# First sums in a tile of their own and weights cast ahead of h at the start; final sums ahead of x1's tiles and row factors read from PSUM at the end

## The chip, the core and the metric

The kernel runs on one core of a Trainium2 chip. The core has a matrix engine (TensorE, "PE" in the profile, with its weight loads as "PEld"), VectorE ("DVE"), ScalarE ("ACT"), GpSimd ("POOL") and SyncE ("SP", used here only to issue DMA transfers). Each engine works through its own queue in order; semaphores tie the queues together. SBUF is the on-chip memory of 128 partitions; PSUM is the accumulator memory that TensorE writes. The metric is the device time of one execution in microseconds; before the change it is 2057.03, the median of three runs (2055.79 to 2059.26).

## What is computed

One step of a layer for 128 context tokens and 256 latent tokens, 384 rows of 2048 channels in all, in float32:

```
mod = silu(cond) @ w_ada + b_ada
sh1, sc1, ga1, sh2, sc2, ga2 = split(mod, 6)
h = rmsnorm(x, norm_pre_mix) * (1 + sc1) + sh1
m, s_f, s_b = mixer(h, ...)
x = x + ga1 * rmsnorm(m, norm_post_mix)
h = rmsnorm(x, norm_pre_ffn) * (1 + sc2) + sh2
ff = (silu(h @ w_ffn_gate) * (h @ w_ffn_up)) @ w_ffn_down
x = x + ga2 * rmsnorm(ff, norm_post_ffn)
```

The mixer (gated linear attention beside a Fourier branch) and the feed-forward products fill the middle of the kernel. The change touches the first two lines of h at the start and the last line at the end.

## The kernel before

Everything is kept transposed: a tile is 128 channels (partitions) by 384 tokens, and there are 16 such tiles of x, numbered k or kb (T = 384, KT = 16, D = 2048). To keep float32 accuracy with the faster rounded type, each operand is split into a rounded part hi and a remainder lo, and a product is made of three matmuls: hi by hi, hi by lo, lo by hi. For a weight tile the split is a copy on ScalarE (`ACT.copy(hi, raw)`, line 224) and a subtraction on VectorE (line 225); for activations it is `split_act` (lines 283 and 284). The order of the instructions on TensorE, ScalarE, VectorE and GpSimd is the order of the program text; SP's is that too in the last part. The bookkeeping of semaphores is automatic: a tile is reused only when its readers are done, and a tile in PSUM is used by one engine at a time.

**Start (lines 316 to 511, "stage A").** SP loads x (`xT`), small columns, and then for each block kb the two halves of a slab of w_ada (128 x 2048 floats each, five buffers), the v weights (`raw`, 128 x 1024, two buffers) and 256 columns of the q weights (`xraw`, two buffers). Behind the loads of blocks 0 and 1 stand five small loads (`wlr`, `coef`, `bgate`, `gnorm`, `selr`, lines 357 to 361), of which `wlr` is used in this stage, by `lrprod`, and the others later. ScalarE squares the 16 tiles of x, VectorE adds them up in two accumulators qsA. TensorE does 10 warming matmuls into `px` (line 432), then sums over the channels (`tok_sum`, line 291: one-column matmuls with ones) into columns of `pmod`, which is a part of the PSUM tile `pgm`. Another part of pgm is `pgv`, in which `gemv` (line 374, 16 matmuls for a block) collects the block's modulation sums. `msx` (line 435) scales the sums, `rsqrt` makes the row factor r0, `rows` (lines 309 and 310) multiplies the identity by it on VectorE three times and spreads it over the partitions with a matmul by ones into px, and ScalarE copies px to `rstd`.

In block kb the loop over kb then does, on TensorE, gemv(kb); up to four products that go through px and are flushed by VectorE (`xprod` for two groups of q columns, line 409, and every fourth block `lrprod`, line 416); `vprod` (line 391) in three parts of six matmuls, for block kb-1: part 0 is hi by hi, part 1 h's hi by the weight's lo, part 2 h's lo by the weight's hi; and a pair of two-column matmuls that folds `ev`, ScalarE's copy of pgv (line 466), into the shift and scale `mods` of the block (lines 476 and 480). VectorE multiplies x by rstd (line 462, into `scr`, called hf), applies mods (line 482), and ScalarE and VectorE split the result into A_hi and A_lo (hT). The block's weights are split after that (`split_w`), and used in the next block.

**End (from line 1205).** In the last chunk of the down projection, `down` adds each product to the accumulator and squares it; the squares are added up in qs[0] on VectorE one tile late (`late`, line 1176), the last one is added by a second matmul source. Then TensorE puts x1's tiles 4, 5 and 8 into PSUM by the identity (`put`, line 1208), sums the squares (line 291), puts 9 and 14, spreads the row factor with `rows` into `prow`, and puts 15. `rr` is ScalarE's copy of prow in SBUF. Each output tile is x1 + acc * factor. Six tiles (4, 5, 8, 9, 14, 15) get the sum on TensorE: VectorE multiplies, TensorE adds the product to py, ScalarE copies py back and stores. Six (0, 1, 6, 7, 12, 13) are multiplied and added on VectorE and stored by SP. Four (2, 3, 10, 11) are multiplied and added on GpSimd and stored by SP. All but the first product read rr from SBUF.

## Time and profile before

| | |
|---|---|
| median of three runs | 2057.03 us |
| profiled execution | 2056.04 us, of which its span 2054.3 us |
| TensorE busy | 2024.7 us, 99% of the span |
| VectorE busy | 1274.9 us, 62% |
| ScalarE busy | 770.1 us, 37% |
| GpSimd busy | 45.4 us, 2% |
| DMA | 373.94 MB moved |

The span runs from the first to the last instruction of the profiled execution; the rest of its time, 1.74 us, lies around it. In a timeline a row has the start and the duration in microseconds, then engine, line, operation, output and inputs, shape and count; a bracket behind it gives the idle time of the engine before it and what ended that. Neighbouring instructions of one kind are merged in a row. In the table of windows each row is a stretch; behind its length come busy time and instructions of TensorE, its weight loads, VectorE, ScalarE and GpSimd, then the granted clock of TensorE as a share of full speed, the DMA engines' mean busy share, and GB/s.

### The profile page before, as it was taken

What the parts mean: (1) busy time and instruction counts of PE and PEld (TensorE: products, weight loads), DVE (VectorE), ACT (ScalarE), POOL (GpSimd) and SP (SyncE); (2) the same over time, 40 slices, a digit from 0 to 9 for tenths busy, and PEclk for the clock granted to TensorE, in tenths of its full rate; (3) what the DMA queues carried; (4) which work ended last, traced back from release to release, by engine and by line L of the source; (5) the groups of instructions that cost most, each with busy time, mean ns of one, the idle gap of its engine ahead of it and who ended that gap; (6) DMA issues with size and microseconds to landing.
All of it is one profiled execution on the core that took longest, in us unless ns stands there. A gap on an engine that the chain in (4) does not pass through costs nothing.

```text
span 2054.3 us, 30097 instructions
## 1 busy us (share of the span) xinstructions
PE 2024.7 (99%) x12214; PEld 1956.1 (95%) x12214; DVE 1274.9 (62%) x1663; ACT 770.1 (37%) x1143; POOL 45.4 (2%) x52
## 2 busy tenths in 40 slices
PE   8999999999999999999999999999999999999998
PEld 5779999999999999978999999999999999999996
DVE  5669787898667778867444555553545454544346
ACT  3233545453346544445333322222222322222234
POOL 0000000000000000022000000000000000000001
PEclk9999999999999999999999999999999999999998
DMA  9978677767646785532444444443444444433332
GB/s 387 354 261 274 206 238 230 240 222 259 202 158 209 257 282 183 187 113 93 154 144 152 146 144 154 144 146 125 150 144 147 151 144 148 148 125 124 123 133 83
DMA packets 112563, 373.94 MB, mean 182 GB/s; under 512 B 13860, under 2 KB 32484, under 8 KB 108328
## 3 DMA queue, kind: packets, MB, share of 16 engines
q1 hardware_dynamic: 111560, 370.84, 52.8%
q8 instruction: 96, 1.57, 0.3%
q10 hardware_dynamic: 864, 1.18, 0.2%
q14 instruction: 43, 0.35, 0.1%
HBM read 358.34 MB, written 13.63 MB: 181 GB/s over the span
## 4 chain that ended last, share of the span: by engine, by line
PE 96%; DVE 2%; DMA 1%; ACT 1%; issue 0%; SPq 0%; DVEq 0%; ACTq 0%
PE pmm L257 66%; PE pdn L257 18%; PE pv L391 3%; PE pf L257 2%; PE pgm L374 1%; PE px L409 1%; DVE yE L1227 0%; PE po L603 0%; PE pmm L1131 0%; DMA Clo<-in_xT 0%; PE pr L538 0%; DMA slab<-in_w_ada 0%; DVE z L1090 0%; PE dl L603 0%; PE px L844 0%
## 5 line engine op out<-in xcount | busy, mean ns | idle before, releaser
L257 PE MATMUL pmm<-A_hi,whi 128*128 128x384 f32 x2480 | 832.6, 336 | 0.0
L257 PE MATMUL pmm<-A_hi,wlo 128*128 128x384 f32 x2480 | 828.9, 334 | 0.0
L257 PE MATMUL pmm<-A_lo,whi 128*128 128x384 f32 x2480 | 828.8, 334 | 0.0
L225 DVE TENSOR_TENSOR wlo<-raw,whi 128x1024 fp32r<-128x1024 f32 x433 | 529.0, 1223 | 433.8 <-ACT whi L224 432.9
L224 ACT CAST whi<-raw 128x1024 fp32r<-128x1024 f32 x436 | 457.7, 1050 | 587.4 <-PE pmm L257 223.2
L257 PEld LDWEIGHTS pmm<-A_hi,whi 128*128 128x128 f32 x2480 | 465.6, 188 | 3.4 <-issue 1.8
L257 PEld LDWEIGHTS pmm<-A_lo,whi 128*128 128x128 f32 x2480 | 465.7, 188 | 0.2
L257 PEld LDWEIGHTS pmm<-A_hi,wlo 128*128 128x128 f32 x2480 | 465.6, 188 | 0.0
L530 DVE SCALAR_TENSOR_TENSOR adacc<-adaw,spad,adacc 128x1024 f32<-128x1024 f32 x240 | 296.9, 1278 | 0.6 <-DMA adaw<-in_w_ada 0.3
L257 PE MATMUL pdn<-hid_hi,whi 128*128 128x384 f32 x704 | 235.2, 334 | 0.0
L257 PE MATMUL pdn<-hid_hi,wlo 128*128 128x384 f32 x704 | 235.1, 334 | 0.0
L257 PE MATMUL pdn<-hid_lo,whi 128*128 128x384 f32 x704 | 235.1, 334 | 0.0
L257 PEld LDWEIGHTS pdn<-hid_hi,whi 128*128 128x128 f32 x704 | 132.2, 188 | 0.4 <-issue 0.4
L257 PEld LDWEIGHTS pdn<-hid_lo,whi 128*128 128x128 f32 x704 | 132.2, 188 | 0.0
L257 PEld LDWEIGHTS pdn<-hid_hi,wlo 128*128 128x128 f32 x704 | 132.2, 188 | 0.0
L283 ACT CAST hid_hi<-hfE 128x384 fp32r<-128x384 f32 x44 | 22.6, 513 | 161.6 <-DVE hfE L1154 161.6
L1154 DVE TENSOR_TENSOR hfE<-sg,pmm 128x384 f32<-128x384 f32 x44 | 24.4, 555 | 82.2 <-PE pmm L257 81.6
L1146 ACT ACTIVATE sg<-pmm 128x384 f32<-128x384 f32 x44 | 21.6, 492 | 133.5 <-PE pmm L257 133.5
L1171 DVE TENSOR_TENSOR Blo<-Blo,pdn 128x384 f32<-128x384 f32 x72 | 39.5, 553 | 46.6 <-PE pdn L257 46.6
L1171 DVE TENSOR_TENSOR Bhi<-Bhi,pdn 128x384 f32<-128x384 f32 x72 | 39.0, 549 | 34.0 <-PE pdn L257 34.0
L257 PE MATMUL pmm<-o_hi,whi 128*128 128x384 f32 x128 | 42.8, 335 | 0.0
L257 PE MATMUL pmm<-o_lo,whi 128*128 128x384 f32 x128 | 42.8, 334 | 0.0
(301 smaller groups left out, 1556.9 us busy)
## 6 DMA issues: line engine op xcount, KB each, us to landing
adaw<-in_w_ada SPq DMA_DIRECT2D x128, 512.0 KB
raw<-in_w_g SPq DMA_DIRECT2D x88, 512.0 KB
raw<-in_w_u SPq DMA_DIRECT2D x88, 512.0 KB
raw<-in_w_d SPq DMA_DIRECT2D x88, 512.0 KB
slab<-in_w_ada SPq DMA_DIRECT2D x32, 1024.0 KB
raw<-in_w_gate SPq DMA_DIRECT2D x64, 512.0 KB
raw<-in_w_in SPq DMA_DIRECT2D x44, 512.0 KB
raw<-in_w_out SPq DMA_DIRECT2D x32, 512.0 KB
```

The source lines that it names most:

```text
L224: ACT.copy(hi, raw)
L225: eng.tensor_sub(lo, raw, hi.bitcast(F32))
L257: PE.matmul(dst, w[wi][:, k * n + n0 : k * n + n0 + P], x[xi][:, k0 + k, :], start=first and k == 0 and j == 0, stop=last and k == kts - 1 ...
L283: ACT.copy(hi, src)
L374: PE.matmul(pgv[q : q + 32, :], spad[:, k, :], slab[k // (KT // 2)][:, k % (KT // 2), :], start=k < 4, stop=k >= KT - 4,)
L391: PE.matmul(pv[2 * t + g], hT[x_][:, kb, t * P : (t + 1) * P], w_[:, g * 512 : (g + 1) * 512], start=kb == 0 and j == 0, stop=kb == KT - 1 ...
L409: PE.matmul(px, w_[:, u * P : (u + 1) * P], hT[x_][:, kb, :], start=j == 0, stop=j == 2)
L530: DVE.scalar_tensor_tensor(acc[:, c, :], w, spad[:, k, c : c + 1], acc[:, c, :], op0=ALU.mult, op1=ALU.add,)
L1146: ACT.activation(sgs[j], p, AF.Silu)
L1154: DVE.tensor_mul(hf, sgs.pop(j), p)
L1171: DVE.tensor_add(acc(k), acc(k), p)
```

## The change

At the start:

- The five small loads are issued in block 4, behind the loads for block 5, instead of ahead of block 2's.
- There are 11 warming matmuls. The channel sums go to px instead of pmod, with 64 columns of ones instead of one; msx reads px. The row factor is spread by three 128x128 matmuls that take r0, broadcast along its columns, as weights and the identity as moving operand; the three scalings on VectorE go.
- gemv's second half of block 0 stands right behind these. In blocks 1 and 2 gemv comes behind vprod's part 0 and the first xprod; part 1 is then made ahead of the pair of two-column matmuls.
- ev is copied ahead of the weights' casts, and the casts ahead of A_hi; the subtractions that make the weights' lo parts come behind A_lo (in block 0, the one for the q columns stays early).
- lrprod runs in blocks 6, 10 and 14 instead of 4, 8 and 12.

At the end:

- The last square but one is not added to qs[0] by VectorE but summed by TensorE as a second source; the last square is summed apart, and VectorE joins the two sums.
- One x1 tile is put ahead of the sums, one ahead of the row factor and one behind it; the other three follow one by one behind the products.
- The row factor is spread as at the start. VectorE's products all read prow in PSUM. Where VectorE also makes the sum, the product goes to a PSUM tile, `pys`. rr is used by GpSimd alone, whose eight operations are issued without a break.
- TensorE has tiles 0, 4, 8, 1, 5, 9; GpSimd 2, 6, 10, 14; VectorE 3, 7, 11, 12, 13, 15.

```diff
-    def split(at=None, eng=DVE, hold=False):
+    def split(at=None, eng=DVE, hold=False, defer=None):
...
                 ACT.copy(hi, raw)
-                eng.tensor_sub(lo, raw, hi.bitcast(F32))
+                sub = lambda: eng.tensor_sub(lo, raw, hi.bitcast(F32))
+                sub() if defer is None else defer.append(sub)
...
-        def split_w(kb):
-
-            split()
+        def split_w(kb, defer):
+
...
-            ACT.copy(hi, raw)
-            DVE.tensor_sub(lo, raw, hi.bitcast(F32))
+
+            if kb == 0:
+                ACT.copy(hi, raw)
+                DVE.tensor_sub(lo, raw, hi.bitcast(F32))
+            split(defer=defer)
+            if kb:
+                ACT.copy(hi, raw)
+                defer.append(lambda: DVE.tensor_sub(lo, raw, hi.bitcast(F32)))
             return take(), (hi, lo)
...
-        SP.dma_start(wlr, a["w_lr"])
...
+        def load_later():
+            SP.dma_start(wlr, a["w_lr"])
...
-        warm(px, 10)
-        tok_sum(pmod[:, 8:11], *qs)
+        warm(px, 11)
+
+        for t in range(3):
+            for n, q in enumerate(qs):
+                PE.matmul(
+                    px[:, t * P : t * P + 64], q[:, t * P : (t + 1) * P], ones[:, 0:64], start=n == 0, stop=n == 1,
+                )
         gemv(0, range(KT // 2))
-        DVE.tensor_scalar_mul(msx, pmod[:, 8:11], 1.0 / D)
+        DVE.tensor_scalar_mul(msx, px[:, 0:T:P], 1.0 / D)
         r0 = pa.tile([P, 3], F32, name="r0")
         rsqrt(r0, msx, 1.0)
-        rows(pb, px, r0, 1)
+        for t in range(3):
+            PE.matmul(px[:, t * P : (t + 1) * P], r0[:, t : t + 1].to_broadcast([P, P]), ident, start=True, stop=True)
+        gemv(0, range(KT // 2, KT))
...
+                if kb == 4:
+                    load_later()
+
+            wait = kb in (1, 2)
+            if kb and not wait:
+                gemv(kb)
             todo = []
-            if kb and kb % 4 == 0:
-                todo.append(lrprod(kb - 4))
+            if kb > 4 and kb % 4 == 2:
+                todo.append(lrprod(kb - 6))
...
+            if wait:
+                vprod(kb - 1, prev[0], (0,))
             pe_x(0)
             hf = scr[:, kb % 8, :]
             DVE.tensor_mul(hf, xn(kb), rstd)
-            if kb == 0:
-                prev = split_w(0)
+            flushes[0]()
+            if wait:
+                gemv(kb)
             ev = pb.tile([P, 256], F32, tag="ev", name="ev")
             ACT.copy(ev, pgv)
-            flushes[0]()
+            lag = []
+            new = split_w(kb, lag)
             if kb:
-                vprod(kb - 1, prev[0], (0,))
+                vprod(kb - 1, prev[0], (1 if wait else 0,))
...
             split_act(hT[0][:, kb, :], hT[1][:, kb, :], hf)
...
+            for sub in lag:
+                sub()
...
-                    if late:
+                    if late and k < KT - 1:
                         DVE.tensor_add(qs[0], qs[0], late.pop())
...
+        put(pe_ks[0], psm, "mm")
+        pst = pss.tile([P, 8], F32, tag="side", name="pstE")
+        prow = pss.tile([P, T], F32, tag="side", name="prowE")
+
+        last_sq = late.pop()
+        tok_sum(pst[:, 0:3], qs[0], *late)
+        tok_sum(pst[:, 4:7], last_sq)
+        r3 = pe.tile([P, 3], F32, name="r3", bufs=1)
+        DVE.tensor_copy(r3, pst[:, 0:3])
+        DVE.tensor_add(r3, r3, pst[:, 4:7])
+        rsqrt(r3, r3, 1.0 / D)
+        put(pe_ks[1], psm, "mm")
...
+        pys = pss.tile([P, T], F32, tag="side", name="pys")
...
+        def on_pool(k):
+            y = pe.tile([P, T], F32, tag="t1", name="yP", bufs=3)
+            POOL.tensor_mul(y, acc(k), rr)
+            POOL.tensor_add(x1(k), x1(k), y)
+
+        def on_pe(n):
+            k = pe_ks[n]
+            y = pe.tile([P, T], F32, tag="hf", name="yE", bufs=4)
+            DVE.tensor_mul(y, acc(k), prow)
+            PE.matmul(py[k], ident, y, start=False, stop=True)
+            if n + 3 < len(pe_ks):
+                put(pe_ks[n + 3], pss, "side")
+            ACT.copy(x1(k), py[k])
+            store(k, ACT)
+
+        for k in pool_ks:
+            on_pool(k)
+        on_pe(0)
+        for n, k in enumerate(dve_ks):
+            DVE.tensor_mul(pys, acc(k), prow)
+            if n + 1 < len(pe_ks):
+                on_pe(n + 1)
+            DVE.tensor_add(x1(k), x1(k), pys)
+            store(k, SP)
+            if n in (1, 3, 4, 5):
+                store(pool_ks.pop(0), SP)
```

More of the change, by code (lines that the diff above doesn't have):

```diff
@@ L488, in tile_step @@
             if kb:
[L489 to L491 removed]
+                if not wait:
+                    vprod(kb - 1, prev[0], (1,))
+                pe_x(2)
+                flushes[2]()
+            for sub in lag:
+                sub()
             if kb:
[L493 removed]
                 vprod(kb - 1, prev[0], (2,))
@@ L1208, in put @@
             PE.matmul(py[k], ident, x1(k), start=True, stop=False)
-        for k in (4, 5, 8):
-            put(k, psm, "mm")
-        pst = pss.tile([P, 4], F32, tag="side", name="pstE")
-        tok_sum(pst[:, 0:3], qs[0], late.pop())
-        r3 = pe.tile([P, 3], F32, name="r3", bufs=1)
-        rsqrt(r3, pst[:, 0:3], 1.0 / D)
-        for k in (9, 14):
-            put(k, pss, "side")
-        prow = pss.tile([P, T], F32, tag="side", name="prowE")
-        rows(pe, prow, r3)
+        pe_ks, pool_ks, dve_ks = [0, 4, 8, 1, 5, 9], [2, 6, 10, 14], [3, 7, 11, 12, 13, 15]
@@ new lines, in tile_step @@
+        put(pe_ks[0], psm, "mm")
[4 more added lines that the diff above has]
+        tok_sum(pst[:, 4:7], last_sq)
+        r3 = pe.tile([P, 3], F32, name="r3", bufs=1)
+        DVE.tensor_copy(r3, pst[:, 0:3])
+        DVE.tensor_add(r3, r3, pst[:, 4:7])
+        rsqrt(r3, r3, 1.0 / D)
+        put(pe_ks[1], psm, "mm")
+        for t in range(3):
+            PE.matmul(
+                prow[:, t * P : (t + 1) * P], r3[:, t : t + 1].to_broadcast([P, P]), ident, start=True, stop=True,
+            )
@@ L1220, in tile_step @@
+        put(pe_ks[2], psm, "mm")
         rr = pe.tile([P, T], F32, tag="rr", name="rrE", bufs=1)
         ACT.copy(rr, prow)
[L1222 to L1235 removed]
```

46 lines of the change are left out of this document (8 added, 38 removed).

## The prediction

> **What bounds the kernel now.** I read the page first (span, busy shares), then the windows of both ends, then the timeline there, engine by engine.
>
> ```profile
> span 2054.3 us, 30097 instructions
> PE 2024.7 (99%) x12214; PEld 1956.1 (95%) x12214; DVE 1274.9 (62%) x1663; ACT 770.1 (37%) x1143; POOL 45.4 (2%) x52
> ```
> ```profile
> 0.00:40.00 40.00, 31.18 (x202) 19.77 (x206) 20.64 (x48) 17.24 (x34) 1.34 (x9) 0.96 0.97 380
> ```
> TensorE is busy for all but 29.6 us of the span. 8.8 of them lie in the first 40 us (40 minus 31.18), where the DMA engines are busy too (share 0.97, the last figure but one). Most of the rest lies behind the last pdn matmul, which is followed at 2030.50 by the first row below; from there on the end hangs on VectorE. So time can come from these two stretches alone.
>
> **The tail, first part: from sums to the row factor.**
>
> ```profile
> 2030.50 1.45 PE L1208 MATMUL py<-Chi,ident 128*128 128x384 f32 x4
> 2032.44 0.28 PE L291 MATMUL pstE<-ones,qsE 128*128 128x1 f32 x2
> 2033.69 1.54 PE L1208 MATMUL py<-Clo,ident 128*128 128x384 f32 x4
> 2033.87 0.26 ACT L302 ACTIVATE r<-pstE,eps_t 128x3 f32<-128x3 f32 x1 [1.78 <-PE pstE L291]
> 2034.16 0.18 DVE L303 RECIPROCAL r<-r 128x3 f32<-128x3 f32 x1 [1.97 <-ACT r L302]
> 2036.06 0.48 ACT L1221 COPY rrE<-prowE 128x384 f32<-128x384 f32 x1 [1.93 <-PE prowE L310]
> 2036.57 0.56 DVE L1227 TENSOR_TENSOR yE<-Bhi,prowE 128x384 f32<-128x384 f32 x1 [1.52 <-ACT rrE L1221]
> ```
> Columns: start, duration, engine, line. A float32 matmul leaves two records, so x4 is two. Three tiles of x1 fill 2030.50 to 2032.44, 0.65 each; six sum matmuls fill 2032.44 to 2033.69, 0.21 each. In the changed order one tile goes first (to 2031.15), then nine sum matmuls. Six need only squares through tile 14, the last three that of tile 15. That square was ready in time for the second sum matmul before (about 2032.6), and VectorE now makes it one addition earlier; it is needed at 2031.15 + 1.26 = 2032.4, so nothing waits. TensorE is through at 2033.05; its reader follows 0.18 later, as at 2033.69 to 2033.87: 2033.2. New on VectorE are a copy and an addition of 128x3 that join the sums, 0.2 each (the reciprocal's 0.18 and a gap). Root (0.29 to the next start) and reciprocal: the factor is there at 2034.15. The three scalings of the identity go. In place of the matmul on them stand three of 128x128 with the broadcast factor as weights. No row has such weights; three at the 0.21 to 0.32 of the rows above and a latency of 0.2 make 0.85, which I take, being nearest in shape, and twice that is the dear end. Then the copy to rr, behind which VectorE's first product stood before (2036.06 to 2036.57, 0.51) and stands again. First product at 2035.55: 1.0 earlier.
>
> **The tail, second part: VectorE's 18 operations.** Twelve products and six additions, before and after.
>
> ```profile
> 2039.22 1.35 DVE L1234 TENSOR_TENSOR Chi<-Chi,yE 128x384 f32<-128x384 f32 x1
> 2046.84 0.54 DVE L1227 TENSOR_TENSOR yE<-Bhi,rrE 128x384 f32<-128x384 f32 x1
> 2047.30 0.55 DVE L1227 TENSOR_TENSOR yE<-Blo,rrE 128x384 f32<-128x384 f32 x1
> 2050.12 0.54 DVE L1227 TENSOR_TENSOR yE<-Blo,rrE 128x384 f32<-128x384 f32 x1
> 2050.69 0.56 DVE L1234 TENSOR_TENSOR Clo<-Clo,yE 128x384 f32<-128x384 f32 x1
> ```
> ```profile
> 2036.61 1.00 POOL L1227 TENSOR_TENSOR yE<-Bhi,rrE 128x384 f32<-128x384 f32 x1 [1083.42 <-ACT rrE L1221]
> 2045.31 1.19 POOL L1234 TENSOR_TENSOR Clo<-Clo,yE 128x384 f32<-128x384 f32 x1
> ```
> While GpSimd works (2036.61 to 2046.50) a VectorE operation with two SBUF inputs takes 1.35; afterwards 0.54. But the product that read prowE from PSUM took 0.56 beside GpSimd. The middle of the kernel shows the same on one operation:
>
> ```profile
> 915.58 3.73 POOL L1073 TENSOR_TENSOR t<-Bhi,rr 128x384 f32<-128x384 f32 x3
> 917.11 0.72 DVE L1084 SCALAR_TENSOR_TENSOR z<-Chi,mods,prow 128x128 f32<-128x128 f32 x2
> ```
> ```profile
> 921.90 1.48 DVE L1084 SCALAR_TENSOR_TENSOR z<-Chi,mods,rr 128x128 f32<-128x128 f32 x2
> ```
> With prow from PSUM 0.72 beside GpSimd, with rr from SBUF 1.48. The change gives each of the 18 one PSUM operand: prow, or the new PSUM tile pys. From start to start an operation then takes 0.47 (2046.84 to 2047.30), and 0.57 if it waits for the one ahead (2050.12 to 2050.69). pys is a single buffer, so a product into it waits for the addition ahead: six steps of 0.57, eleven of 0.47, and 0.56 for the last operation make 9.15. That is 2035.55 to 2044.7, where before it was 2036.57 to 2051.25, 14.7. No row has a product written to PSUM; I take the same time, and 0.1 more for each of six as the dear end.
>
> [...]
>
> GpSimd has four products and four additions as before: 9.9 from 2035.55 is 2045.45, and sooner if VectorE no longer holds it up.
>
> **The stores.**
>
> ```profile
> 2051.00:2052.00 1.00, 0.00 (x0) 0.00 (x0) 0.25 (x1) 0.00 (x0) 0.00 (x0) 0.50 1.02 366
> 2053.00:2054.00 1.00, 0.00 (x0) 0.00 (x0) 0.00 (x0) 0.00 (x0) 0.00 (x0) 0.50 0.01 2
> ```
> ```profile
> 2048.34 0.33 SPq L1235 DMA_DIRECT2D out_yT<-Chi  x1
> ```
> The span ends 3.05 after the last addition (2051.25) and 1.3 after the last data (2053.0). Sixteen stores of 0.197 MB at 366 GB/s are 8.6 us of data; the first can be issued at 2037.4 (first product, matmul and copy behind it) and its data move some 0.9 later, so the data end no sooner than 2046.9 and the span than 2048.2. By the last addition it is 2044.7 + 3.05 + 0.33, as a second store stands behind it on SP: 2048.1. By GpSimd at its old pace, 2045.45 + 3.05 = 2048.5. I take 2048.15 for 2054.3: **6.15 less**; dear ends of the two unknown costs, 4.7 (0.85 and 0.6 more), best 6.5 (rows 0.35 cheaper).
>
> **The head.**
>
> ```profile
> 13.62 1.74 PE L291 MATMUL pgm<-ones,qsA 128*128 128x1 f32 x12 [1.08 <-DVE qsA L429]
> 16.43 0.16 DVE L435 TENSOR_SCALAR msx<-pgm 128x3 f32<-128x3 f32 x1 [2.24 <-PE pgm L374]
> 19.55 1.85 PE L374 MATMUL pgm<-slab,spad 128*32 128x256 f32 x16
> 21.48 0.37 ACT L466 COPY ev<-pgm 128x256 f32<-128x256 f32 x1
> 23.07 1.93 PE L374 MATMUL pgm<-slab,spad 128*32 128x256 f32 x32 [0.56 <-DVE mods L480]
> 23.75 0.51 ACT L283 CAST A_hi<-scr 128x384 fp32r<-128x384 f32 x1 [1.90 <-DVE scr L482]
> ```
> The sums end at 15.36, yet msx starts at 16.43, behind the gemv half that writes the same tile. Written to px, they let it start at 15.5; root and reciprocal to 16.2. The row matmuls follow the gemv half, 16.45 to 17.25; the copy to rstd ends at 17.75, the second gemv half at 18.2 (0.95 where it took 1.85 at half clock). ev is next on ScalarE, at 18.25, ahead of the two weight casts; from ev to A_hi 2.27 as before (21.48 to 23.75), and 0.15 for the small weights' subtraction that now stands before mods: A_hi at 20.65, done at 21.2. That is **3.1 earlier**.
>
> Less of it reaches TensorE, for two reasons. Loads first:
>
> ```profile
> 32.61 1.07 PE L374 MATMUL pgm<-slab,spad 128*32 128x256 f32 x16 [0.77 <-DMA slab<-in_w_ada]
> 39.46 1.93 PE L374 MATMUL pgm<-slab,spad 128*32 128x256 f32 x32
> 47.16 1.93 PE L374 MATMUL pgm<-slab,spad 128*32 128x256 f32 x32
> ```
> and from the chain of waits, the two products behind a gemv:
>
> ```profile
> 41.39 0.72 PE px L409 x3
> 42.11 1.39 PE pv L391 x6
> ```
> The second half of block 2's slab landed at 32.6. The loads land in order at about 400 GB/s; without the five small ones (309 KB by their shapes, 0.8 us) it lands at 31.8. A block's loads (2.75 MB) take 6.7, so slab 3 is there at 38.5. Then the clock, the third figure from the right:
>
> ```profile
> 14.44:17.85 3.41, 1.93 (x25) 1.26 (x24) 0.94 (x5) 0.30 (x1) 0.00 (x0) 0.99 1.02 408
> 17.85:21.25 3.40, 3.28 (x18) 1.10 (x18) 0.76 (x3) 1.59 (x3) 0.00 (x0) 0.51 1.00 417
> 21.25:24.66 3.41, 2.35 (x40) 1.46 (x36) 2.79 (x7) 1.02 (x3) 0.00 (x0) 1.00 1.01 393
> ```
> A stretch of 3.4 us with TensorE busy for 1.93, half of it one-column sums, was followed by one at half clock. In the changed order the thin stretch is 17.85 to 21.25: 0.35 of gemv, a pair of two-column matmuls, and then the wait for A_hi. So half clock is likely from 21.25. Block 1 from 21.2: vprod 1.4, xprod 0.7, gemv 1.9, 4.0 together, of which half clock makes 5.7; its other 3.7 end at 30.6. Block 2 takes 7.7 (39.46 to 47.16), and 0.25 because its xprod now stands ahead of gemv, before the small weights' remainders are there: 38.55, slab 3 landing just in time. Before, it was 39.46: **0.9 less**. At full clock it would be 36.85 and then a wait for slab 3, as if started at 37.55: 1.9 less. Should the loads land 1.2 later, 0.3 is lost.
>
> [...]
>
> From block 3 on TensorE's order is the old one. The weights' casts now stand ahead of A_hi on ScalarE, 1.45 a block; I cost them at nothing, for ScalarE idles there:
>
> ```profile
> ACT A_hi L283 <- DVE scr L482: 50.5, 16, 3.3
> ```
> That is 3.2 a block; without this gap it would be up to 1.45 a block. VectorE's subtraction of the large weights stays behind A_lo. The small loads stand behind block 4's on SP, ahead of slab 6: TensorE's 7.7 a block against the loads' 6.7 has made 2 us of cover by then; without it, block 6 would wait the 0.8 that block 2 did.
>
> **The sum.** The profiled execution took 2056.04 for its span of 2054.3. 2056.04 - 6.15 - 0.9 = **2049.0**. The median shown, 2057.03, is 1.0 above that execution; this goes into the range.
>
> **The rivals.** (a) GpSimd slows VectorE in spite of the PSUM operand, or pys does. In GpSimd's 9.9 us VectorE does eight operations at 1.27 (start to start, the 1.35 above), then ten at 0.47: 14.7, as before; only 1.0 and 0.9 remain: 2054.1. The prow rows speak against it; for it, that no row has a PSUM output. 0.08. (b) The loads are the head's bound and it gains nothing: 2049.9. The DMA share speaks for it, TensorE's wait of only 0.77 on them against. 0.12. (c) The clock stays full in the head: 2048.0. 0.20. (d) Slower: the raw weights land late, ScalarE stands at their cast, and A_hi behind it is late for the next vprod. It decides once A_hi is over 4 us late (6.3 after gemv starts; needed at 7.7 + 2.6), so raw weights 8 us behind their slab. To end above 2060.2 it must cost the 7.05 gained and 4.1 more, 0.75 in each of 15 blocks: 2060.3. A raw load (0.52 MB) follows its slab by 1.3, which speaks against. 0.04. Forecast: 0.56.
>
> **The numbers.** 0.2%, about what a measurement can tell from no change here, is 4.1: faster is below 2052.9. The forecast, (b) and (c), 0.88, lie there, less 0.04 for all dear ends at once (4.7 and a loss of 0.3: 2051.6) with a median 1.3 or more above: faster 0.84, same 0.12 with (a), slower 0.04. The range runs from 2056.04 - 6.5 - 2.0 = 2047.5 to 2051.6, with the 1.0 between execution and median on each side, and 0.3 more above: 2046.5 to 2052.9.
>
> **What would show it.** VectorE's 18 at 0.47 to 0.57 from start to start beside GpSimd; the first product 5.05 after the first x1 tile (6.1 before); stores at full share until 1.3 before the end; A_hi's first cast near 20.65; a half-clock stretch behind it, or none; block 3's gemv near 38.6 and 7.7 a block from there. Products of 1.3 beside GpSimd, or blocks of 8 us and more, would make the prediction wrong.

## The result, and the profile after

The changed kernel took 2048.17 us, the median of five executions (2047.69 to 2052.53), against 2057.03, also of five executions (2055.79 to 2059.26): ratio 0.9958, interval 0.9947 to 0.997. Eight more executions of the same kernel, later, had a median of 2052.77 (2050.39 to 2055.57), ratio 0.9975 (0.9965 to 0.9985). All thirteen together have a median of 2050.86. The predicted 2049.0 lies between the medians of the two sets. The profiled execution is the shortest of the thirteen, 2047.69 for a span of 2045.9, and the sum below is made against it.

From the page of the changed kernel:

```profile
span 2045.9 us, 30092 instructions
PE 2021.4 (99%) x12230; PEld 1956.7 (96%) x12230; DVE 1267.9 (62%) x1658; ACT 770.4 (38%) x1143; POOL 43.6 (2%) x52
```
The two stages in which the prediction looked for time are these, in the same views as before. The first 40 us, from the windows:

```profile
0.00:40.00 40.00, 33.27 (x231) 21.84 (x232) 20.66 (x47) 17.66 (x36) 1.34 (x9) 1.00 0.96 382
```
The start in the timeline; the matmuls with `slab` are gemv:

```profile
15.61 0.16 DVE L448 TENSOR_SCALAR msx<-px 128x3 f32<-128x3 f32 x1 [1.32 <-PE px L444]
16.50 0.93 PE L452 MATMUL px<-ident,r 128*128 128x128 f32 x6
20.83 0.51 ACT L284 CAST A_hi<-scr 128x384 fp32r<-128x384 f32 x1 [0.57 <-DVE scr L506]
23.51 1.93 PE L382 MATMUL pgm<-slab,spad 128*32 128x256 f32 x32
31.26 0.45 PE L417 MATMUL px<-A_hi,wlo 128*128 128x384 f32 x1 [0.24 <-DVE wlo L346]
37.62 1.93 PE L382 MATMUL pgm<-slab,spad 128*32 128x256 f32 x32
45.32 1.93 PE L382 MATMUL pgm<-slab,spad 128*32 128x256 f32 x32
```
TensorE is busy 2.1 us more of the first 40 (33.27 for 31.18). A_hi's first cast is at 20.83 where it was at 23.75. No gemv has a wait for a slab any more, and block 3's starts at 37.62, 1.84 earlier. From there on a block takes 7.70 (37.62 to 45.32), as before.

The end, first from the last chunk to VectorE's first product, then VectorE's and GpSimd's work:

```profile
2027.67 0.81 PE L1234 MATMUL py<-Chi,ident 128*128 128x384 f32 x2
2028.31 0.28 PE L292 MATMUL pstE<-ones,qsE 128*128 128x1 f32 x2
2031.36 0.93 PE L1250 MATMUL prowE<-ident,r 128*128 128x128 f32 x6 [0.23 <-DVE r L304]
2032.33 0.48 ACT L1255 COPY rrE<-prowE 128x384 f32<-128x384 f32 x1 [1.23 <-PE prowE L1250]
2032.84 0.56 DVE L1271 TENSOR_TENSOR yE<-Bhi,prowE 128x384 f32<-128x384 f32 x1 [1.54 <-ACT rrE L1255]
...
2033.32 0.56 DVE L1282 TENSOR_TENSOR pys<-Bhi,prowE 128x384 f32<-128x384 f32 x1
...
2034.24 0.55 DVE L1285 TENSOR_TENSOR Chi<-Chi,pys 128x384 f32<-128x384 f32 x1
...
2041.50 0.55 DVE L1285 TENSOR_TENSOR Clo<-Clo,pys 128x384 f32<-128x384 f32 x1
```
```profile
2032.89 1.00 POOL L1265 TENSOR_TENSOR yP<-Bhi,rrE 128x384 f32<-128x384 f32 x1 [1082.54 <-ACT rrE L1255]
...
2040.07 1.00 POOL L1266 TENSOR_TENSOR Clo<-Clo,yP 128x384 f32<-128x384 f32 x1
```
All 18 operations of VectorE now take 0.55 to 0.56, though GpSimd works beside all but the last; before, eight took up to 1.35. GpSimd's take 1.00 each, and are through 8.2 after the first, not 9.9. The windows of the stores, with the DMA share and GB/s last:

```profile
2032.84:2035.60 2.76, 2.25 (x8) 1.35 (x8) 2.72 (x6) 0.48 (x1) 2.63 (x3) 1.00 0.00 0
2035.60:2044.60 9.00, 4.56 (x13) 1.74 (x11) 6.28 (x13) 2.39 (x5) 5.23 (x6) 0.98 0.97 349
2044.60:2045.90 1.30, 0.00 (x0) 0.00 (x0) 0.00 (x0) 0.00 (x0) 0.00 (x0) 0.50 0.01 4
```
Between marks that both traces have, the span of 2054.3 became 2045.9 as follows:

| from | to | before | after | difference | predicted |
|---|---|---|---|---|---|
| start | block 3's gemv | 39.46 | 37.62 | -1.84 | -0.9; at full clock -1.9 |
| | first matmul of the Fourier part | 488.87 | 487.89 | -0.98 | 0 |
| | first x1 tile | 1502.17 | 1502.16 | -0.01 | 0 |
| | VectorE's first product | 6.07 | 5.17 | -0.90 | -1.02 |
| | end of the last addition | 14.68 | 9.21 | -5.47 | -5.53 |
| | end of the span | 3.05 | 3.85 | +0.80 | +0.40 |

The second row wasn't in the prediction at all. It is the wait in the bracket here, of the kernel before and of the changed one:

```profile
528.33 0.67 PE L844 MATMUL px<-cd,fs 128*128 128x257 f32 x2 [1.34 <-issue]
```
```profile
525.51 0.67 PE L870 MATMUL px<-cd,fs 128*128 128x257 f32 x2 [0.37 <-issue]
```

### The profile page after: what moved, and what is told of

Its sections match the earlier page's. It is cut to its first block, busy times and chain, and to the rows that moved or that the text cites. A ratio compares the mean times of both kernels' runs of the same rounds, so it can differ in the third digit from the quotient of the medians.

```text
span 2045.9 us, 30092 instructions
## 1 busy us (share of the span) xinstructions
PE 2021.4 (99%) x12230; PEld 1956.7 (96%) x12230; DVE 1267.9 (62%) x1658; ACT 770.4 (38%) x1143; POOL 43.6 (2%) x52
## 4 chain that ended last, share of the span: by engine, by line
PE 95%; DVE 2%; DMA 1%; ACT 1%; issue 0%; SPq 0%; DVEq 0%; ACTq 0%
PE pmm L258 66%; PE pdn L258 18%; PE pv L399 3%; PE pf L258 2%; PE pgm L382 1%; PE px L417 1%; PE po L629 0%; DMA xraw<-in_w_x 0%; PE pr L564 0%; DMA Clo<-in_xT 0%; DVE z L1116 0%; PE dl L629 0%; DVE z L1110 0%; PE px L870 0%; DVE A_lo L1129 0%
## 5 line engine op out<-in xcount | busy, mean ns | idle before, releaser
L1180 DVE TENSOR_TENSOR hfE<-sg,pmm 128x384 f32<-128x384 f32 x44 | 24.4, 555 | 83.1 <-PE pmm L258 82.5
```

What stands on the lines that cost most here:

```text
L1180: DVE.tensor_mul(hf, sgs.pop(j), p)
```

## The experiments

They ran in three groups of four, in the order below (the small loads, gemv first and the last two kernels are the third group), each group on another chip; the kernel before had medians of 2057.74, 2057.57 and 2057.56 beside them. Executions of one kernel spread over 2 to 8 us, so whether a step does what was said of it is read from the stages of the profile, and the medians are only given beside them. My theory was the prediction's sum with the head at full clock; the rival in each case is in the expectation. The diffs are against the changed kernel, that of the end alone against the kernel before.

**The start alone** (the last part of `down` and all from the first `put` on as in the kernel before):

```diff
-                    if late and k < KT - 1:
+                    if late:
...
-        put(pe_ks[0], psm, "mm")
+        for k in (4, 5, 8):
+            put(k, psm, "mm")
...
-        for t in range(3):
-            PE.matmul(
-                prow[:, t * P : (t + 1) * P], r3[:, t : t + 1].to_broadcast([P, P]), ident, start=True, stop=True,
-            )
+        rows(pe, prow, r3)
```


> The start of the changed kernel with the end of the old one. The theory that the start gives 1.85 us by itself: block 3's gemv at 37.6 us in the profile and 2055.2 us (2057.0 - 1.85); 2054.2 if the 1.0 us that the first Fourier block gave in the changed kernel comes from the start's shift. Rival, the loads are the start's bound: block 3's gemv at 39.5 and 2057.0. If a half-clock stretch follows A_hi, as the prediction had it, block 3's gemv at 38.6 and 2056.2.

Measured 2055.92 (ratio 0.9992, 0.9983 to 1.0002). Block 3's gemv starts at 37.69, at the full clock as in the changed kernel, and the end is the old one to 0.02 us (6.07, 14.68 and 3.03 in the three stages). By the median the start is worth 1.8, within an interval that reaches to nothing.

**The end alone** (the start as in the kernel before). The edit puts the changed kernel's end into the kernel before.

```diff
-                    if late:
+                    if late and k < KT - 1:
...
-            ys[k] = pe.tile([P, T], F32, tag=tag, name="yE", bufs=bufs)
-            eng.tensor_mul(ys[k], acc(k), r)
+            DVE.tensor_mul(y, acc(k), prow)
```


> The start of the old kernel with the end of the changed one. The theory that the end gives 5.6 us by itself: first product 5.2 us after the first x1 tile, VectorE's 18 operations in 9.2 us, 2051.4 us (2057.0 - 5.6), and TensorE's wait at the first Fourier block stays at 1.3 us. Rival, the two ends help each other: more than 2052.4 here. If the wait at the first Fourier block is scatter from run to run, it may be anything from 0.4 to 1.4 us here too.

Measured 2053.3 (0.9979, 0.997 to 0.9988). VectorE's 18 operations, in the windows:

```profile
2035.38:2044.58 9.20, 6.81 (x19) 3.09 (x18) 8.99 (x18) 2.87 (x6) 7.88 (x8) 1.00 0.67 241
```
They take 9.20, with 5.17 ahead of them and 3.82 behind: the end's 5.6 us don't need the new start. By its median, though, this kernel gains only 4.4 and lies above the 2052.4 that the rival named; the median alone leaves the rival standing, and it is the stages of the profile that speak against it (the profiled execution, the shortest of ten, took 2050.22). Block 3's gemv starts at 38.93 here, with the old start, where the one profile of the kernel before has 39.46. The medians of the two halves, 1.8 and 4.4, add up to 6.2, less than the 8.9 of the changed kernel's first five executions. This is what made me measure that kernel again.

**No PSUM operand** (products read rr, the product for a sum lies in SBUF) and **products in PSUM's row only** (`pys` alone in SBUF):

```diff
-        pys = pss.tile([P, T], F32, tag="side", name="pys")
+        pys = pe.tile([P, T], F32, tag="rr2", name="pys", bufs=1)
...
-            DVE.tensor_mul(y, acc(k), prow)
+            DVE.tensor_mul(y, acc(k), rr)
...
-            DVE.tensor_mul(pys, acc(k), prow)
+            DVE.tensor_mul(pys, acc(k), rr)
```
The second kernel has the first of these three edits alone.

> The changed kernel, but VectorE's products read the row factor's copy in SBUF, and the products for its own sums go to an SBUF tile; order and count of all operations stay. Theory, two SBUF operands beside GpSimd cost 1.27 us from start to start: the 18 operations take 14.7 us for 9.2, GpSimd's eight take 9.9 us for 8.2, and the time is 2052.9 us (2048.2 + 5.5 - 0.8, since the stores no longer pile up at the end). Rival, the new order of the operations gives the gain and not the PSUM operand: 2048.2 to 2048.7 us.

> The changed kernel, but the products for VectorE's own sums go to an SBUF tile instead of the PSUM tile pys; all products still read the row factor in PSUM. Theory, only an operation with two SBUF inputs contends: the twelve products stay at 0.55 us, the additions beside GpSimd take 1.35, four or five of six, so the 18 take about 12.6 us for 9.2 and the time is 2050.8 us (2048.2 + 3.4 - 0.8). Rival, an SBUF output beside one SBUF input is enough to contend: no change against the changed kernel, whose products already have that, or 2048.2 us if pys matters for nothing.

Measured 2057.54 (1.0, 0.9991 to 1.001) and 2054.11 (0.9983, 0.9973 to 0.9992). Of the kernel without PSUM operands, a few operations of both engines, from the timeline:

```profile
2037.55 1.20 POOL L1266 TENSOR_TENSOR Chi<-Chi,yP 128x384 f32<-128x384 f32 x1
2037.81 1.35 DVE L1271 TENSOR_TENSOR yE<-Bhi,rrE 128x384 f32<-128x384 f32 x1
2038.71 1.31 POOL L1265 TENSOR_TENSOR yP<-Bhi,rrE 128x384 f32<-128x384 f32 x1
```
and of the kernel with `pys` alone in SBUF:

```profile
2038.55 0.55 DVE L1271 TENSOR_TENSOR yE<-Bhi,prowE 128x384 f32<-128x384 f32 x1
2039.01 1.14 DVE L1285 TENSOR_TENSOR Chi<-Chi,pys 128x384 f32<-128x384 f32 x1
```
The same order of instructions with all operands in SBUF has VectorE at 1.23 to 1.35 again where GpSimd works beside it, and GpSimd at 1.19 to 1.37 in place of 1.00. VectorE works 15.44 us, and the end takes 24.4 (23.8 in the kernel before), against 18.2. So the PSUM operands make 6.2 us, more than the end's whole gain; the new order without them would lose 0.6. In these two kernels it is the second input that counts, not the output: with the row in PSUM a product into SBUF takes 0.55, and the addition of two SBUF tiles after it 1.14 to 1.38 beside GpSimd (work 12.29, expected 12.6). The medians lie 4.6 and 3.3 above the expected ones. In the profiled executions block 3's gemv is 1.3 to 1.5 late (a half clock at the start) and TensorE's wait at the Fourier part 1.7 to 1.8 longer than in the changed kernel's first profile, of which more below; and the 0.8 that I had expected back from the stores didn't come in either (3.80 and 3.90). In the second the rest of the middle is 1.7 longer too, with a half-clock stretch behind that wait (a Fourier matmul of 257 columns takes 1.04 there, and 0.60 in the changed kernel).

**The changed kernel again.**

> The changed kernel once more, for more executions and a second profile. The head alone took 1.8 us off and the tail alone 4.4, 6.2 together, so if the two add up the median is near 2051, with single executions spread over some 5 us: the half-clock stretch behind the A_hi casts costs 1.4 us at block 3's first gemv wherever it falls there (two of four profiles of this head so far), and PE's wait for the first Fourier block has been anywhere from 0.37 to 2.2 us. Median 2049.5 to 2051.5. Rival: the 2048.17 of the first five executions is the kernel's own time, 2047.7 to 2048.9, and the two parts give more together than apart. The tail is the same in either case: first product 5.17 us after the first x1 tile, 9.2 us of VectorE work, 3.85 us from the last add to the end.

Measured 2052.77 (2050.39 to 2055.57): above the 2049.5 to 2051.5 that was expected, and far from the rival's 2047.7 to 2048.9. The profiled execution took 2054.47. Its start has block 3's gemv at 37.55, its end 5.18, 9.20 and 3.90: all as in the first profile. The 6.8 us more are in two places. The first, with the chain that leads to it, engine by engine:

```profile
514.11 8.79 SPq L899 DMA_DIRECT2D wr<-in_w_br_four  x12
526.86 1.04 ACT L224 CAST whi<-raw 128x1024 fp32r<-128x1024 f32 x1 [12.05 <-DMA raw<-in_w_in]
527.94 1.23 DVE L225 TENSOR_TENSOR wlo<-raw,whi 128x1024 fp32r<-128x1024 f32 x1 [9.48 <-ACT whi L224]
529.66 0.55 DVE L925 TENSOR_TENSOR fs<-fs,pmm 128x384 f32<-128x384 f32 x1
529.73 1.20 PE L870 MATMUL px<-cd,fs 128*128 128x257 f32 x2 [4.64 <-issue]
```
The same chain in the first profile of the changed kernel:

```profile
522.63 1.05 ACT L224 CAST whi<-raw 128x1024 fp32r<-128x1024 f32 x1 [8.40 <-DMA raw<-in_w_in]
525.44 0.56 DVE L925 TENSOR_TENSOR fs<-fs,pmm 128x384 f32<-128x384 f32 x1
```
SP issues twelve loads of 4 KB in 8.79 us (8.05 in the first profile), and the raw weights behind them are late. ScalarE waits for them (12.05 and 8.40), VectorE waits for ScalarE's cast, the sums fs stand behind that subtraction in VectorE's queue, and TensorE's first Fourier matmul starts 0.1 behind the first of the two operations that make fs (it ends at 529.63 and 525.41, and the matmul starts at 529.73 and 525.51). In one execution it waited 4.64, in the other 0.37. The second place is behind it:

```profile
528.10:534.90 6.80, 5.17 (x16) 4.65 (x17) 6.70 (x7) 4.07 (x12) 0.95 (x1) 0.52 0.67 239
```
The clock is at half (0.52) for 6.8 us after the wait; from here to the next stage it took 379.0 us instead of 376.5.

**The sums behind x1's tiles again** (three tiles ahead of the sums, the last square but one added by VectorE):

```diff
-        put(pe_ks[0], psm, "mm")
+        for n in range(3):
+            put(pe_ks[n], psm, "mm")
...
-        last_sq = late.pop()
-        tok_sum(pst[:, 0:3], qs[0], *late)
-        tok_sum(pst[:, 4:7], last_sq)
+        tok_sum(pst[:, 0:3], qs[0], late.pop())
```


> PSUM parts of the tail stay, the first step is undone: the three x1 tiles stand ahead of the final sums again and VectorE adds the last square into qs before the sums, as in the kernel before. The time from the first x1 tile to the first product was 6.07 us before and is 5.17 in the changed kernel. If the 0.90 between them is this step, 6.0 to 6.1 stands here again and the time is 0.9 us above the changed kernel's of the same chip. Rival: the three row products wait for something else (the square root's chain on ScalarE and VectorE), then 5.2 to 5.4 and no change of time. VectorE's work stays at 9.2 and the end at 3.85 in both.

Measured 2050.83 (0.9964, 0.9952 to 0.9977).

```profile
2033.47 0.18 DVE L304 RECIPROCAL r<-r 128x3 f32<-128x3 f32 x1 [1.97 <-ACT r L303]
2035.18 0.56 DVE L1266 TENSOR_TENSOR yE<-Bhi,prowE 128x384 f32<-128x384 f32 x1 [1.54 <-ACT rrE L1250]
```
The first x1 tile is at 2029.81 here, so the reciprocal is done, at 2033.65, 3.84 after it (3.64 in the changed kernel, 3.84 before), and the first product is at 5.37. The step is worth 0.20, not 0.90. The other 0.70 is the stretch from the reciprocal's end to the first product, 1.53 in both kernels with broadcast weights and 2.23 with the scaled identities. The 6.0 to 6.1 that would have stood here if the step were the whole 0.90 is out, and 5.37 lies in the rival's 5.2 to 5.4. The median can't show 0.20: it lies 1.9 below that of the changed kernel on the same chip, where 0.9 above was expected.

The end took 4.82 behind the last addition here. The windows show a granted clock of 0.51 over most of VectorE's work:

```profile
2034.70:2041.50 6.80, 5.71 (x9) 3.20 (x10) 6.21 (x13) 1.41 (x3) 6.04 (x7) 0.51 0.39 141
```
TensorE's six tiles come late, and their stores with them: ScalarE issues the last at 2045.68, 1.3 behind the last addition, where in the changed kernel's first profile the last one was issued 0.1 ahead of it.

**The stores in the order in which tiles are ready:**

```diff
-            if n in (1, 3, 4, 5):
+            if n == 4:
+                store(k, SP)
+                store(pool_ks.pop(0), SP)
+            elif n in (1, 2, 3):
+                store(k, SP)
+                if n != 3:
+                    store(pool_ks.pop(0), SP)
+            else:
+                store(k, SP)
+                if n == 0:
+                    store(pool_ks.pop(0), SP)
```


> The stores alone: GpSimd's tiles go out as soon as they are added (order 3, 2, 7, 6, 11, 10, 12, 13, 14, 15) in place of after VectorE's next tiles, the sums as in the changed kernel. From the last add to the end it was 3.85 us in the changed kernel and 3.05 before; the stores moved 16 tiles within 8.5 us at some 366 GB/s with a hole of half a microsecond after the first of them. If the order makes the hole, the data end 0.25 to 0.5 us earlier and the end comes 3.35 to 3.6 us after the last add, the time 0.3 to 0.5 us lower. Rival: the engines are filled by then whatever the order (16 tiles of 196 KB at 366 GB/s are 8.6 us from the first store on), 3.8 us and no change; or GpSimd's tiles come later than SP reaches them, SP waits, and the end is later by up to 0.5 us.

Measured 2049.02 (0.9955, 0.994 to 0.9971).

```profile
2039.20:2047.90 8.70, 5.13 (x15) 2.26 (x13) 6.24 (x13) 2.39 (x5) 5.20 (x6) 1.00 1.00 362
```
The data now move without a hole, 8.70 us at 362 GB/s in place of 9.00 at 349, and the end comes 12.79 after the first product, not 13.06. The hole was the order's, and it cost 0.27. The median, of four executions, lies 3.8 below that of the changed kernel on the same chip, which 0.27 doesn't explain; and in the profiled execution a half-clock stretch (0.62 granted from 2036.41 to 2039.20; the row matmuls took 1.22 for 0.93) made the first product 0.29 late, so that from the first x1 tile to the end it took 18.25, as before the step (18.23). What is left is one sum: 2.8 from the first product to the first data, 8.7 of data, 1.3 behind them. VectorE's work, 9.2, is no longer the bound.

**The first sums back in the modulation's tile:**

```diff
-        warm(px, 11)
+        warm(px, 10)
...
-        for t in range(3):
-            for n, q in enumerate(qs):
-                PE.matmul(
-                    px[:, t * P : t * P + 64], q[:, t * P : (t + 1) * P], ones[:, 0:64], start=n == 0, stop=n == 1,
-                )
+        tok_sum(pmod[:, 8:11], *qs)
```


> The head's first sums go back into the modulation's PSUM tile with one column each, with ten warming matmuls as in the kernel before; all else is the changed kernel's. If this step made the 0.9 us by which the sums' tail ahead of h got shorter, the first block of A_hi ends 0.7 to 1.0 us later than the changed kernel's 20.83, and block 3's first gemv starts at 38.5 to 38.7 us at the full clock, or 39.9 to 40.1 where the half-clock stretch falls behind A_hi; the time is 0.9 us above the changed kernel's. Rival: A_hi is set by the slabs and by the casts ahead of h, A_hi at 20.8 to 21.0, and no change.

Measured 2054.36 (0.9981, 0.9972 to 0.999).

```profile
18.29 1.62 PE L448 MATMUL px<-ident,r 128*128 128x128 f32 x6 [0.90 <-DVE r L304]
24.08 0.51 ACT L284 CAST A_hi<-scr 128x384 fp32r<-128x384 f32 x1 [0.61 <-DVE scr L502]
```
```profile
15.10:21.90 6.80, 5.77 (x42) 2.91 (x42) 0.90 (x3) 0.83 (x3) 0.00 (x0) 0.53 1.02 417
```
A_hi is at 24.08, 3.3 later, where 0.7 to 1.0 was expected. The row matmuls come 1.8 later (18.29 for 16.50), since they wait for a whole gemv half, and this half ran at half clock, 1.93 for 1.07, as did the next. So the direction holds. Block 3's gemv is at 42.41, where 38.5 to 38.7 or 39.9 to 40.1 was expected. At full clock I estimate the step at the 1.0 of the gemv half that lies between the sums and msx (15.50 to 16.50 in the changed kernel); how much of the 3.3 is the clock's chance in this one execution isn't separated.

**The small loads early, and gemv first.** In the first, `load_later()` stands ahead of block 2's loads again; in the second, blocks 1 and 2 have gemv ahead of their products:

```diff
-            wait = kb in (1, 2)
+            wait = False
```


> The five small loads (309 KB) go back to their old place on SP, ahead of block 2's slab; all else is the changed kernel's. If the loads' order gave the 0.8 us that the prediction counted, block 2's and block 3's slabs land 0.8 us later: a wait of up to 0.8 us for a slab stands again in block 2 or 3, and block 3's first gemv starts 0 to 0.8 us later than the 37.5 to 37.6 (full clock) or 38.9 to 39.1 (half-clock stretch behind A_hi) of the changed kernel's profiles. Rival: with two blocks' products ahead of their gemv the slabs have time enough, no wait for a slab appears, and nothing changes. Medians of single executions spread over 5 us here, so the place is read from the profile.

> Blocks 1 and 2 of the head run their gemv ahead of the products of the block before it, as the kernel before did; all else is the changed kernel's. If that order matters, TensorE stands at block 1's or block 2's gemv for its slab (block 2's second half landed at 32.6 in the kernel before), and block 3's first gemv starts 1.0 to 1.4 us later: 38.6 to 39 at the full clock. Rival: block 1's gemv fills TensorE's 1.9 us wait for A_hi, the slab has landed by then, and block 3's gemv starts up to 1 us earlier; the half-clock stretch behind A_hi is then less likely too.

Measured 2051.8 (0.9972, 0.9962 to 0.9983) and 2053.26 (0.9977, 0.9968 to 0.9986). gemv of blocks 1 and 3 with gemv first:

```profile
23.34 1.79 PE L382 MATMUL pgm<-slab,spad 128*32 128x256 f32 x16 [1.34 <-DMA slab<-in_w_ada]
39.46 1.93 PE L382 MATMUL pgm<-slab,spad 128*32 128x256 f32 x32
```
With the small loads early no gemv waits for a slab; block 3's starts at 39.31, 0.2 above the other profiles with a half-clock stretch there (38.8 to 39.1), and A_hi was as much late already. The place of the small loads is worth nothing that shows. With gemv first block 1 stands 1.34 for its slab, and block 3 starts 0.3 to 0.7 later than in those profiles (it had half clock too, 23.5 to 27.0); 1.0 to 1.4 was expected. The order took the loads off the path.

**The Fourier part's small loads on GpSimd's queue:**

```diff
-                    SP.dma_start(wr[r : r + 1, :].rearrange("p (i c) -> p i c", c=P), src.rearrange("i p c -> p i c"))
+                    POOL.dma_start(wr[r : r + 1, :].rearrange("p (i c) -> p i c", c=P), src.rearrange("i p c -> p i c"))
```


> The changed kernel with the 24 small loads of w_br_four ahead of and inside the first Fourier block on GpSimd's queue, which is idle there, in place of SP's. In the profiles SP takes 8.1 to 8.8 us for the first 12 of them, 4 KB each, the DMA engines stand nearly empty meanwhile (share 0.03), and the raw weights behind them are late: ScalarE waits 8.4 to 12 us for them and TensorE 0.37 to 4.64 us at the first Fourier block, once with a half-clock stretch behind it (376.5 us from there to pw became 379.0). If these loads are the cause, TensorE's wait there is 0.3 or none, the half-clock stretch behind it goes, ScalarE's wait falls to below 3 us, and the median is 1 to 3 us below the changed kernel's (2049.5 to 2051.5 on this chip) with a narrower spread. Rival: the wait is for something else (the constants cd, or VectorE's fs), 0.4 to 4.6 as before and no change.

Measured 2048.52 (2047.27 to 2049.68; 0.9952, 0.9937 to 0.9967).

```profile
521.63 0.55 DVE L925 TENSOR_TENSOR fs<-fs,pmm 128x384 f32<-128x384 f32 x1
525.01 0.59 PE L870 MATMUL px<-cd,fs 128*128 128x257 f32 x2
```
fs is done 2.8 us before TensorE comes to it (522.2 and 525.01), and the first Fourier matmul has no wait in its row. ScalarE's casts no longer wait for the raw weights; it waits 7.36 for the small loads themselves, ahead of a cast at 525.12 that TensorE doesn't wait for here. The twelve profiles with these loads on SP all have the wait, the two with them on GpSimd's queue haven't: this shows the cause of the second row of the table. The median has no run of the changed kernel in the same group to be compared with; its two sets have 2048.17 and 2052.77.

**These together with a second row tile for ScalarE's copy:** the GpSimd queue, the order of stores, and

```diff
+        prow2 = pss.tile([P, T], F32, tag="side", name="prow2E")
+        for t in range(3):
+            PE.matmul(
+                prow2[:, t * P : (t + 1) * P], r3[:, t : t + 1].to_broadcast([P, P]), ident, start=True, stop=True,
+            )
...
-        ACT.copy(rr, prow)
+        ACT.copy(rr, prow2)
```


> The changed kernel with three more steps: the Fourier block's small loads on GpSimd's queue, the stores in the order in which the tiles are ready (which ended 3.59 us behind the last add where the changed kernel's three profiles have 3.82 to 3.90), and a second PSUM tile with the row factor for ScalarE's copy, so that VectorE's first product needn't stand behind that copy (0.51 us in every profile so far). If the two engines are held apart only by the shared tile, the first product comes 4.65 to 4.75 us after the first x1 tile instead of 5.17, and as the data end 8.6 us behind the first store, the end comes 0.5 us earlier by this and 0.25 by the stores' order; with the Fourier block 1.7 to 3.7 us in all: a median of 2046.5 to 2049. Rival: the first product waits for the three more row matmuls or for the tile pool instead (5.2 and more), and only the Fourier step is left.

Measured 2048.11 (2046.57 to 2050.12; 0.9949, 0.9937 to 0.9962).

```profile
2033.44 0.56 DVE L1276 TENSOR_TENSOR yE<-Bhi,prowE 128x384 f32<-128x384 f32 x1 [1.47 <-PE prowE L1250]
...
2034.72 0.48 ACT L1260 COPY rrE<-prow2E 128x384 f32<-128x384 f32 x1 [2.96 <-PE prow2E L1255]
2035.28 0.99 POOL L1270 TENSOR_TENSOR yP<-Bhi,rrE 128x384 f32<-128x384 f32 x1 [1084.25 <-ACT rrE L1260]
```
The first product no longer stands behind ScalarE's copy; its row names the row matmuls as what it waited for. It comes 5.11 after the first x1 tile, where 4.65 to 4.75 was expected. But the copy now comes after three more matmuls, and GpSimd starts 1.84 after VectorE instead of 0.05. GpSimd's stores are late, and the end, 19.3 us from the first x1 tile, is 1.0 longer than in the changed kernel (18.2), part of both by a half-clock stretch that began over the row matmuls (they took 1.38, and 0.93 in the changed kernel). The third step fails here. The median is no clearly better than with the Fourier step alone (2048.11 and 2048.52). This kernel and the one before it together have nine executions from 2046.57 to 2050.12, and the changed kernel's thirteen run from 2047.69 to 2055.57. But their intervals of the ratio lie largely within that of the changed kernel's first five executions, and the later eight ran on another chip, so that they are faster than the changed kernel is likely and not shown.

## Why the prediction was right

The mechanism of the end held, in each of its steps, and it carries the forecast: 5.5 to 5.6 of 6.15 us came, in both profiles of the changed kernel and with the old start too.

- *From sums to the row factor, 1.02 predicted.* 0.90 came: 0.20 from the sums' place and their two sources (0.19 in the working, factor at 3.65 after the first tile; 3.64 measured), 0.70 from the broadcast weights. The row matmuls, for which no row stood, were taken at 0.85 with their latency; they took 0.97 (2031.36 to the copy at 2032.33), and 1.02 from the reciprocal's end.
- *VectorE's 18 operations.* 9.15 predicted, 9.20 to 9.21 in every kernel with both PSUM operands. A product written to PSUM took what one written to SBUF did, 0.55 to 0.56; the dear end wasn't needed. Rival (a) is out: 1.35 came back only with a second SBUF input.
- *The stores, the term that was mis-sized.* 3.45 behind the last addition was predicted and 3.85 measured. I took the end from the last addition and held the bound by the data (8.6 us from the first store on) to be the same moment. It is the data that decide, and to their bound came a hole of 0.27 that the order of SP's stores makes, and 0.1 to 0.2 of small pieces.
- *The start.* Both branches of the prediction occur. Of the nine profiles with the changed start as it is, four have block 3's gemv at 37.5 to 37.7 (full clock, predicted 37.55) and five at 38.8 to 39.1 (half-clock stretch behind A_hi, predicted 38.55). The forecast's half clock had 0.56 and rival (c) 0.20; the first profiled execution was rival (c)'s. One and the same start gave both, and what decides between them no run shows. Inside the branch two errors cancelled: the predicted wait for slab 3 never came, so rival (b) is out, but block 2 took 8.39 where 7.95 was counted, since its xprod took 0.49 longer by its wait for the weights' remainder, where 0.25 was allowed, and its other products 0.2 longer; and block 1 began 0.2 late. The 0.8 counted for the small loads' place doesn't show.
- *Casts ahead of A_hi cost nothing.* Right: 7.70 a block from block 3 on, and rival (d) is out.
- *What was misread.* Of the 29.6 us in which TensorE is idle in the kernel before, 8.8 lie at the start. "Most of the rest" does not lie behind the last pdn matmul: 9.6 do, and 11.2 lie in the middle.

```profile
40.00:2030.50 1990.50, 1979.34 (x11982) 1929.85 (x11975) 1237.22 (x1591) 748.43 (x1099) 34.48 (x35) 1.00 0.53 179
2030.50:2054.30 23.80, 14.21 (x39) 6.45 (x38) 16.99 (x25) 4.42 (x10) 9.57 (x8) 0.74 0.37 132
```
So "from these two stretches alone" doesn't follow, and "From block 3 on TensorE's order is the old one" took the middle as fixed. It has a wait that differs from execution to execution, 1.34 in the one profile of before that the prediction had, and 0.18 to 4.64 in the eleven others that left these loads alone. The first profile of the changed kernel got 0.98 of its 8.4 by that, which is chance. The rest of the middle isn't fixed either: from the first Fourier matmul to the first x1 tile the fourteen profiles took 1501.88 to 1504.69, and 1503.94 in one whose wait was only 0.18 (small loads early); what makes that is open.
- *How near the number came.* The first profile's 8.4 is the 7.05 of the sum, less 0.58 at the end, 0.94 more by the full clock at the start, and the 0.98. So that 2048.17 came so near 2049.0 is in part luck. The sum from the median of all executions of the kernel before, 2057.57, would be 2050.5, and the thirteen executions have 2050.86. (The bound of rival (d), 2060.2, counts its 4.1 from the profiled execution, where the 2052.9 counts it from the median; from there it would be 2061.1.)

A count for a usual execution then is:

- the end 5.6, or 4.6 to 5.1 where a half-clock stretch lies over it, as in two of the seven profiles with the changed end;
- the start 0.3 to 0.7 with the half-clock stretch and 1.8 to 1.9 without, against the 39.46 of the one profile of before, and 0.5 less against the 38.93 of the kernel with the end alone, whose start is the old one too;
- the Fourier part nothing, on average.

The medians of all executions differ by 6.7 (2057.57 and 2050.86).

## What to carry to other kernels

Where VectorE and GpSimd work side by side, try one input in PSUM for each of VectorE's two-input operations: such an operation took 0.55 to 0.56 here, and 1.14 to 1.38 with both in SBUF. That alone was worth 6.2 us, and reordering without it nothing. When the work before the stores shrinks, count the end again from the first store: bytes over rate, plus the time to the first data and behind the last. Before a stage is called fixed, look whether its waits hang on a queue with many tiny loads: twelve of 4 KB, issued in 8.05 to 8.79 us, held up half a megabyte of weights here.

## What was not expected of the hardware

The half clock came back where TensorE had been partly idle, and not at the same place in every execution. In the kernel with the sums behind x1's tiles, whose start is the changed one:

```profile
17.40:20.80 3.40, 1.61 (x21) 0.87 (x20) 2.00 (x6) 2.21 (x5) 0.00 (x0) 0.99 1.02 419
20.80:24.20 3.40, 2.95 (x7) 2.37 (x8) 2.16 (x3) 0.40 (x1) 0.00 (x0) 0.51 1.01 407
```
1.61 us busy in a stretch of 3.40 was followed by one at half clock (0.51). In the changed kernel's first profile the granted clock changes at 9.83, 907.53, 917.77 and 2044.17 us, in that of the kernel before at 7.53, 17.77, 21.18, 908.64, 918.88 and 2041.87. In both these moments lie whole multiples of 3.413 us apart: from 9.83 to 907.53 it is 897.70, 263 of them. Stretches of that length, counted on from 9.83 (an estimate, as the clock stays full there), hold in the changed kernel's start:

```profile
16.66:20.07 3.41, 2.38 (x26) 1.52 (x26) 1.28 (x4) 2.01 (x4) 0.00 (x0) 1.00 1.05 430
20.07:23.49 3.42, 2.09 (x9) 1.60 (x9) 2.81 (x6) 0.70 (x2) 0.00 (x0) 1.00 0.99 411
```
Here the same idle time fell on two stretches, and neither was followed by half clock. Counted in this way, by estimate again, the thinnest stretch held 1.17 to 1.68 us of busy time in the five profiles of the changed start where half clock followed, and 1.91 to 2.26 in the four where it didn't. In the kernel before, 2.02 was followed by it (the prediction's 1.93, with its edges taken 0.09 later), so the busy time alone doesn't tell the two outcomes apart. The first change of the clock was at 9.58 to 10.13 in the four, and at 7.09 to 8.70 in the five; what sets it no run shows. The end had it as well: in five profiles with the new end a half-clock stretch lay over it (putting a tile of x1 took up to 1.49 us for 0.81), and there the first product came up to 0.63 later (5.80 with the GpSimd queue) or the stores ended up to 0.97 later (4.82).

Loads issued by SP took 0.67 to 0.73 us each where twelve small ones stood in a row (8.05 and 8.79 for twelve), twice the 0.33 of a single load of 512 KB in the same part of the kernel, with the DMA engines at a share of 0.02 to 0.06 from some 3 us after the first of them.
